# Norm's products of w_o's two parts and of the state space output placed some units further on in PE's order; norm of tokens on DVE alone

## The chip, the cores and the metric

The kernel runs on one NeuronCore of a Trainium2 chip. Its engines work beside each other, each on a queue of its own in a fixed order: PE (matrix products, out of PSUM, the accumulator memory), DVE (vector operations), ACT (activations and copies), POOL (a second vector engine), SP (here: DMA issue). They meet in semaphores. The metric is device time of one execution in microseconds (us). Three runs of the kernel before gave 1786.41, 1787.78 and 1782.34; the median is 1786.41.

## What is computed

One step of a decoder layer for 1024 prompt tokens and 32 sample tokens (1056 columns, T): a mixer with a state space part, cross-attention to 256 memory tokens, and a gated FFN, each with an RMS norm ahead. What matters here:

```python
def rmsnorm(x, g):
    xf = x.astype(F32)
    var = jnp.mean(xf * xf, axis=-1, keepdims=True)
    return (xf * lax.rsqrt(var + EPS) * g.astype(F32)).astype(x.dtype)
...
    y = rmsnorm(y * jax.nn.silu(z.astype(F32)), norm_g)          # state space output
...
    h = h + jnp.concatenate([ya, yb, yc], axis=-1) @ W['w_out'][l]
    h = h + mem_attention(rmsnorm(h, W['norm_mem'][l]), mem_k[l], mem_v[l], W['w_mem_q'][l], W['w_mem_o'][l])
    u = rmsnorm(h, W['norm_ffn'][l])
    h = h + (jax.nn.silu(u @ W['w_ffn_gate'][l]) * (u @ W['w_ffn_up'][l])) @ W['w_ffn_down'][l]
```

All in float32. A product of float32 matrices is made of three products of float32r parts: each operand is split into a high part (ACT copies it) and a low part (DVE subtracts), and high x high, low x high and high x low are summed in PSUM.

## The kernel before

Activations lie with the 1024 features on the partitions (8 tiles `h` of 128 x 1056) and the tokens along the row, so a token's sum of squares runs over partitions. An RMS norm is therefore made on PE in two steps with DVE between. **pv**: the squares, summed over the eight tiles into `acc`, are multiplied by a column of ones, which gives one column of sums per 128 tokens. DVE and ACT turn these into `nr`, 1/rms (`newton`: a root on ACT, a reciprocal and four small operations on DVE). **pb**: `nr` is broadcast by PE transposes, and ACT copies the result to `rbc`, which the activations are multiplied with.

PE and SP execute in the order in which the program is written; ACT, DVE and POOL are put in order by a scheduler when the program is built, and that order is fixed from then on. Where side work stands in PE's order is set by a clock of its own: `tick()` is called at fixed points of the product loops, and a generator that was handed to `spawn` goes on after as many ticks as the number that it yields. In the loop over w_out a unit of 24 matmuls is two ticks; in the loop over w_o's second part a unit of 12 matmuls is two ticks; in the first gate tile 12 matmuls of `st` are one tick.

Three norms are concerned.

- The state space output (`rstd`, L192, called at L879). Its factor is applied after the product with w_out: `z_pairs` are multiplied by w_out unscaled, and `evac` (L901) multiplies what comes out by `rbc`. All three column groups (c = 0, 1, 2; 352 columns) make pv together, two ticks after the loop begins, and pb some ticks later. `nv`, `nr` and `nq` come from the pool `sp`, which has two buffers of each.
- The FFN's norm, first half of the columns of both halves of the tokens (`normed(0, ...)`, L1169). It runs beside the second half of w_o's second part: the loop of L1288 adds units of 12 matmuls to h (`mm`, evacuated by DVE at L1296, three PSUM buffers), squares h on ACT (L1299) and sums on POOL (L1300).
- The same for the second half (`normed(1, ...)`, from `beside`, L1435). It runs beside the first tile of gate and up (L1440 and on): PE makes eight products `st`, four on the first half (c = 0), then four on the second, 48 matmuls each, from `X`, the split, normalised activations. The last two of four are multiplied to `tm` by DVE (L1462).

`normed` goes through four quarters k. For each, ACT scales two tiles of h by the norm's gain (L1175), `un` is multiplied by `rbc` (L1176: one tile on DVE, one on POOL), and `pair` splits the result into x (L1163 on ACT, L1164 on DVE). The first gate tile needs x of all four quarters within its first 12 matmuls, of each half anew. `sums` (L1186) then makes, on DVE and ACT, the sums that the next tiles need: these use a Strassen scheme with seven products (B11, T2, B21, T3, T1, T4, B22). The weights for all this are split on ACT and DVE too (L1258, L1259).

Of the kernel before, what the change touches and what calls it, by code (L numbers as in the profile page):

```python
# [12 lines left out]
OP = mybir.AluOpType  # L13
# [46 lines left out]
def hybrid_step(ctx, tc, xT, memT, consts_d, masks_d, wbd_d, poolw_d, spool_d, w_kv, w_xbc, w_dt, w_lg, w_pool, w_z, h0_d,  # L60
                w_out1, w_out2, w_q, kc_d, vc_d, w_o, w_gu, w_down,
                yT, ktT, vN, smallo, pssd, sssd):
    nc = tc.nc
# [11 lines left out]
    def nm(s):  # L75
        cnt[0] += 1
        return f"{s}{cnt[0]}"

    def slot(dt=F32, name="s"):
        return sl.tile([P, T], dt, tag="slot", name=nm(name))  # L80
# [5 lines left out]
    def spawn(gen):  # L86
        step(gen)

    def step(gen):
        n = next(gen, None)  # L90
        if n is not None:
            heapq.heappush(queue, (now[0] + n, next(order), gen))
# [6 lines left out]
    def drain():  # L99
        while queue:  # L100
            tick()
# [3 lines left out]
    def mmps():  # L105
        return ps.tile([P, CW], F32, tag="mm", name=nm("mm"), bufs=3)

    def smps(shape=(P, 512), name="sm"):
        return ps.tile(list(shape), F32, tag="sm", name=nm(name), bufs=sm_bufs)
# [37 lines left out]
    def unit(out, w, xs, cols, kk):  # L147
        whi, wlo = w
        for k in range(kk):
            a, b = k * P, k * P + P  # L150
            xh, xl = xs[k]
            nc.tensor.matmul(out, whi[:, a:b], xh[:, cols], start=k == 0, stop=False)  # L152
            nc.tensor.matmul(out, whi[:, a:b], xl[:, cols], start=False, stop=False)  # L153
            nc.tensor.matmul(out, wlo[:, a:b], xh[:, cols], start=False, stop=k == kk - 1)  # L154
            if k == kk // 2 - 1:
                tick()
        tick()

    def ch(c):
        return slice(c * CW, (c + 1) * CW)  # L160
# [7 lines left out]
    def cc(name, i=None, n=1):  # L168
        a, b = COFF[name]
        return cst[:, a:b] if i is None else cst[:, a + i:a + i + n]  # L170
# [10 lines left out]
    def newton(r, v, q):  # L181

        nc.scalar.activation(q, v, AF.Sqrt)
        nc.vector.reciprocal(r, q)
        nc.vector.tensor_tensor(q, r, r, op=OP.mult)
        nc.vector.tensor_tensor(q, q, v, op=OP.mult)
        nc.vector.tensor_scalar(q, q, -0.5, 1.5, op0=OP.mult, op1=OP.add)
        nc.vector.tensor_tensor(r, r, q, op=OP.mult)
# [3 lines left out]
    def rstd(c, acc, rbc, n0=0, n1=2):  # L192

        ready[c] = False
        yield n0
        pv = smps(name="pv")
        w = (P, P, CW - 2 * P)
        for t in range(3):
            nc.tensor.matmul(pv[:w[t], t:t + 1], acc[:, t * P:t * P + w[t]], ones[:, :1], start=True, stop=True)
        v = sp.tile([P, 3], F32, tag="nv", name=nm("nv"))  # L200
        r = sp.tile([P, 3], F32, tag="nr", name=nm("nr"))
        q = sp.tile([P, 3], F32, tag="nq", name=nm("nq"))
        nc.gpsimd.memset(v, 1.0)
        nc.vector.tensor_scalar(v[:, :2], pv[:, :2], 1.0 / DM, EPS, op0=OP.mult, op1=OP.add)
        nc.vector.tensor_scalar(v[:w[2], 2:], pv[:w[2], 2:3], 1.0 / DM, EPS, op0=OP.mult, op1=OP.add)
        newton(r, v, q)
        yield n1
        pb = smps(name="pb")
        for t in range(3):
            nc.tensor.transpose(pb[:, t * P:t * P + w[t]], r[:w[t], t:t + 1].to_broadcast([w[t], P]), ident[:w[t], :w[t]])  # L210
        nc.scalar.activation(rbc[:, ch(c)], pb[:, :CW], AF.Copy)
        ready[c] = True
# [137 lines left out]
    for m in range(8):  # L350
        beside(m)
        pk = ps.tile([P, 256], F32, tag="mm", name=nm("pk"), bufs=3)
        unit(pk, kvw[m], mpairs, slice(0, 256), KD)
        kt = tp.tile([P, 256], F32, tag="cy", name=nm("kt"), bufs=5, padded_shape=[P, CY])
        nc.scalar.activation(kt, pk, AF.Copy)
        nc.scalar.dma_start(ktT[m * P:(m + 1) * P, :], kt)
# [477 lines left out]
    z_acc = []  # L834
# [38 lines left out]
    rbc = rp.tile([P, T], F32, tag="rbc", name="rbc_ssd")  # L873
# [2 lines left out]
    h = [bp.tile([P, T], F32, tag="h", name=nm("h"), bufs=8) for _ in range(8)]  # L876
    nc.sync.dma_start(h[0], xT[:P])
    for c in range(NCH):
        spawn(rstd(c, z_acc[c], rbc, 2, 2))  # L879
    ypairs = []  # L880

    def reload():
# [49 lines left out]
    with ExitStack() as at:  # L932
# [193 lines left out]
        rbc = rp.tile([P, T], F32, tag="rbc", name="rbc_ffn")  # L1126
# [5 lines left out]
    def both(t, c):  # L1132

        return t.rearrange("p (s t) -> p s t", s=2)[:, :, c * HB:(c + 1) * HB]

    def rstd2(c):

        pv = smps(name="pv")
        cuts = [(2 * s + i, s * TH + c * HB + i * P, P) for s in range(2) for i in range(2)]
        cuts += [(4 + s, s * TH + c * HB + 2 * P, HB - 2 * P) for s in range(2)]  # L1140
        for i, a, n in cuts:
            nc.tensor.matmul(pv[:n, i:i + 1], acc[:, a:a + n], ones[:, :1], start=True, stop=True)
        v, r, q = (sp.tile([P, 6], F32, tag=t, name=nm(t)) for t in ("nv", "nr", "nq"))
        nc.gpsimd.memset(v, 1.0)
        nc.vector.tensor_scalar(v[:, :4], pv[:, :4], 1.0 / DM, EPS, op0=OP.mult, op1=OP.add)
        nc.vector.tensor_scalar(v[:HB - 2 * P, 4:], pv[:HB - 2 * P, 4:6], 1.0 / DM, EPS, op0=OP.mult, op1=OP.add)
        newton(r, v, q)
        yield 2
        for s in range(2):
            pb = smps(name="pb")  # L1150
            a0 = s * TH + c * HB
            for i, a, n in cuts:
                if a0 <= a < a0 + HB:
                    nc.tensor.transpose(pb[:, a - a0:a - a0 + n], r[:n, i:i + 1].to_broadcast([n, P]), ident[:n, :n])
            nc.scalar.activation(rbc[:, a0:a0 + HB], pb[:, :HB], AF.Copy)
# [6 lines left out]
    def pair(hi, lo, src):  # L1162
        nc.scalar.activation(hi, src, AF.Copy)  # L1163
        nc.vector.tensor_tensor(lo, src, hi.bitcast(F32), op=OP.subtract)  # L1164

    def four(t):
        return t.rearrange("p (s t) -> p s t", s=4)

    def normed(c, n0, n1):  # L1169
        yield n0  # L1170
        yield from rstd2(c)
        for k in range(4):
            UN[k, c] = u4 = four(slot(name="un"))
            for j in range(2):
                nc.scalar.activation(u4[:, 2 * j:2 * j + 2], both(h[k + 4 * j], c), AF.Copy, scale=cc("gffn", k + 4 * j))  # L1175
                (nc.gpsimd if j else nc.vector).tensor_tensor(u4[:, 2 * j:2 * j + 2], u4[:, 2 * j:2 * j + 2], both(rbc, c),  # L1176
                                                              op=OP.mult)
            for j in range(2):
                x = four(slot(F32R, "x"))
                pair(x[:, :2], x[:, 2:], u4[:, 2 * j:2 * j + 2])  # L1180
                for i in range(2):
                    X[f"B{j + 1}{i + 1}", k, c] = x[:, i], x[:, 2 + i]
            if n1 and k < 3:
                yield n1
# [26 lines left out]
    def hold():  # L1211

        m = len(held)
        if m % 2 == 0:
            hold.at = [(wp if m < 4 else fp).tile([P, DM], F32R, tag=t if m < 4 else "b" + t, name=nm(t), bufs=2) for t in ("whi", "wlo")]
        hi, lo = (t[:, m % 2 * 512:m % 2 * 512 + 512] for t in hold.at)
        split_into(w_o[1, m], 512, hi, lo)
        held.append((hi, lo))
# [45 lines left out]
    def fetch():  # L1264
        x = next(gen, None)
        if x is not None:
            batches.append(x)
        return x
# [19 lines left out]
    for c in range(2):  # L1288
        for m in range(8):
            while len(held) < min(m + 2, 8):  # L1290
                hold()
            for s in range(2):
                cols = slice(s * TH + c * HB, s * TH + (c + 1) * HB)
                p = mmps()[:, :HB]
                unit(p, held[m], op1, cols, 4)
                nc.vector.tensor_tensor(h[m][:, cols], h[m][:, cols], p, op=OP.add)  # L1296
            if m:
                sq = fp.tile([P, 2, HB], F32, tag="sq2", name=nm("sq"), bufs=2)
                nc.scalar.activation(sq, both(h[m], c), AF.Square)  # L1299
                nc.gpsimd.tensor_tensor(both(acc, c), both(acc, c), sq, op=OP.add)  # L1300
            else:
                nc.scalar.activation(both(acc, c), both(h[m], c), AF.Square)
            if c and m % 2:
                fetch()
            if c:
                nc.scalar.dma_start(h_dram[:, m, :], h[m])
        if c == 0:
            spawn(normed(0, 4, 6))
    drain()
    ps_.close()  # L1310
    sm_bufs = 2
# [121 lines left out]


    def beside():  # L1435
        yield from normed(1, 2, 1)
        yield 1
        yield from sums(0, 2)
        yield from sums(1, 2)
# [286 lines left out]
```

## Time and profile before

| | |
|---|---|
| median of three runs | 1786.41 us |
| the profiled execution | 1788.4 us |
| its span, first to last instruction | 1786.6 us |
| mean granted clock of PE | 0.99 |
| POOL's mults at L1176, between 1030 and 1081 us | 8, of 1.32 to 1.85 us each |

A row of the timeline gives start, duration, engine, line, operation, output tile and inputs; in square brackets the idle time of the engine before it and what ended it. A row of the waits gives who waited for whom, total us, times and the longest. A row of the windows gives the stretch, its length, busy time (and instructions) of PE, PE's weight loads, DVE, ACT and POOL, PE's granted clock, and the DMA share and rate.

### The profile page before, as it was taken

The page shows a single profiled execution, that of the slowest core. Times are in us where ns is not written, and L with a number is a line of the kernel's source. Part 1 is how long each engine was busy: PE and PEld are TensorE (multiplying, and loading weights), DVE is VectorE, ACT ScalarE, POOL GpSimd, SP SyncE. Part 2 cuts the span into 40 slices and gives each one's busy share as a digit, 9 for nine tenths or more (in the row PEclk, how much of TensorE's full clock was granted, in tenths as well). Part 3 has the DMA queues.
Part 4 walks back from the last instruction along what each step waited for, and adds up shares of the span by engine and source line. Part 5 has one row for each costly group of instructions (what it writes and reads, how often), then busy time and mean ns, then how long its engine had stood idle before and what let it go on. Part 6 is the DMA issues. An engine that isn't in the chain of part 4 may idle for free.

```text
span 1786.6 us, 31851 instructions
## 1 busy us (share of the span) xinstructions
PE 1723.3 (96%) x12307; PEld 1672.8 (94%) x12307; DVE 1131.4 (63%) x2045; ACT 811.7 (45%) x1650; POOL 593.1 (33%) x618
## 2 busy tenths in 40 slices
PE   8899999999999999999999989999999999899997
PEld 7799988888999999999999979999999999899896
DVE  4887877676844534455566479555555556786855
ACT  6546665678634313245565255222322224343344
POOL 2312446554232322212221243433343332211435
PEclk9999999999999999999999989999999999999998
DMA  9112123341320522233344230233322224543322
GB/s 344 68 48 68 65 70 92 107 145 57 125 83 31 210 84 84 79 131 121 116 140 165 90 144 32 85 115 107 105 100 91 96 90 170 199 164 112 118 72 98
DMA packets 106503, 197.51 MB, mean 111 GB/s; under 512 B 15344, under 2 KB 33392, under 8 KB 106352
## 3 DMA queue, kind: packets, MB, share of 16 engines
q1 hardware_dynamic: 94832, 173.54, 28.6%
q10 hardware_dynamic: 11520, 21.94, 3.3%
q8 instruction: 97, 1.59, 0.4%
q14 instruction: 54, 0.44, 0.1%
HBM read 151.54 MB, written 43.89 MB: 109 GB/s over the span
## 4 chain that ended last, share of the span: by engine, by line
PE 77%; DVE 10%; ACT 4%; issue 3%; POOL 3%; DMA 3%; SPq 0%; ACTq 0%; DVEq 0%; POOLq 0%
PE mm L152 12%; PE mm L154 12%; PE mm L153 12%; PE st L1325 10%; PE st L1326 10%; PE st L1327 10%; DVE cy L503 1%; PE poa L1082 1%; PE pss L1064 1%; ACT seg L558 1%; DVE xd L1371 1%; PE st L1453 1%; PE st L1455 1%; PE st L1454 1%; DMA xd<-hid_dram 1%
## 5 line engine op out<-in xcount | busy, mean ns | idle before, releaser
L152 PE MATMUL mm<-uh,whi 128*128 128x352 f32 x960 | 321.1, 334 | 1.1 <-ACT cy L501 1.1
L1325 PE MATMUL st<-x,whi 128*128 128x264 f32 x1120 | 318.9, 285 | 1.0 <-ACT tm L1505 0.5
L1326 PE MATMUL st<-x,whi 128*128 128x264 f32 x1120 | 318.1, 284 | 0.0
L1327 PE MATMUL st<-x,wlo 128*128 128x264 f32 x1120 | 318.0, 284 | 0.0
L154 PE MATMUL mm<-uh,wlo 128*128 128x352 f32 x960 | 311.1, 324 | 0.0
L153 PE MATMUL mm<-ul,whi 128*128 128x352 f32 x960 | 311.0, 324 | 0.0
L1325 PEld LDWEIGHTS st<-x,whi 128*128 128x128 f32 x1120 | 210.7, 188 | 1.6 <-ACT tm L1505 0.7
L1327 PEld LDWEIGHTS st<-x,wlo 128*128 128x128 f32 x1120 | 210.7, 188 | 0.0
L1326 PEld LDWEIGHTS st<-x,whi 128*128 128x128 f32 x1120 | 210.6, 188 | 0.0
L152 PEld LDWEIGHTS mm<-uh,whi 128*128 128x128 f32 x960 | 182.0, 190 | 5.7 <-issue 1.7
L153 PEld LDWEIGHTS mm<-ul,whi 128*128 128x128 f32 x960 | 182.5, 190 | 2.5
L154 PEld LDWEIGHTS mm<-uh,wlo 128*128 128x128 f32 x960 | 181.7, 189 | 0.0
L1325 PE MATMUL st<-xd,whi 128*128 128x264 f32 x504 | 144.6, 287 | 13.7 <-ACT w L1551 7.1
L1326 PE MATMUL st<-xd,whi 128*128 128x264 f32 x504 | 144.0, 286 | 0.0
L1327 PE MATMUL st<-xd,wlo 128*128 128x264 f32 x504 | 143.7, 285 | 0.0
L1258 ACT ACTIVATE whi<-as 128x512 fp32r<-128x512 f32 (+1 forms) x128 | 74.6, 584 | 139.5 <-PE st L1326 96.3
L1258 ACT ACTIVATE whi<-ar 128x512 fp32r<-128x512 f32 (+1 forms) x104 | 60.8, 588 | 150.4 <-PE st L1326 84.3
L123 ACT ACTIVATE whi<-wraw 128x512 fp32r<-128x512 f32 x128 | 77.5, 627 | 106.2 <-PE mm L153 80.1
L1243 POOL TENSOR_TENSOR as<-ar 128x512 f32<-128x512 f32 (+1 forms) x32 | 53.0, 1655 | 205.8 <-DVE wlo L1259 181.6
L124 DVE TENSOR_TENSOR wlo<-wraw,whi 128x512 fp32r<-128x512 f32 x128 | 96.0, 767 | 23.6 <-ACT whi L123 23.5
L1325 PEld LDWEIGHTS st<-xd,whi 128*128 128x128 f32 x504 | 95.6, 190 | 15.2 <-ACT w L1551 7.3
L957 POOL TENSOR_TENSOR kvlo<-kvraw,kvhi 128x512 fp32r<-128x512 f32 x32 | 41.4, 1295 | 163.2 <-ACT kvhi L956 125.3
(460 smaller groups left out, 4437.6 us busy)
## 6 DMA issues: line engine op xcount, KB each, us to landing
ar<-w_gu SPq DMA_DIRECT2D x88, 256.0 KB, 4.1
hid_dram<-tm SPq DMA_DIRECT2D x71, 264.0 KB, 2.1
xd<-hid_dram SPq DMA_DIRECT2D x63, 264.0 KB, 4.9
ar<-w_down SPq DMA_DIRECT2D x48, 192.0 KB, 3.2
h_dram<-h ACTq DMA_DIRECT2D x16, 528.0 KB, 3.0
h<-h_dram SPq DMA_DIRECT2D x16, 528.0 KB, 6.3
seg<-acs_dram SPq DMA_DIRECT2D x32, 256.0 KB, 3.9
wraw<-w_out SPq DMA_DIRECT2D x32, 256.0 KB, 3.6
```

Source lines behind the costliest of these rows:

```text
L123: nc.scalar.activation(hi[:, a:b], raw, AF.Copy)
L124: nc.vector.tensor_tensor(lo[:, a:b], raw, hi[:, a:b].bitcast(F32), op=OP.subtract)
L152: nc.tensor.matmul(out, whi[:, a:b], xh[:, cols], start=k == 0, stop=False)
L153: nc.tensor.matmul(out, whi[:, a:b], xl[:, cols], start=False, stop=False)
L154: nc.tensor.matmul(out, wlo[:, a:b], xh[:, cols], start=False, stop=k == kk - 1)
L503: nc.vector.scalar_tensor_tensor(y[:, :n], raw[:, j:j + n], w[j], y[:, :n], op0=OP.mult, op1=OP.add)
L957: eng.tensor_tensor(lo, src, hi.bitcast(F32), op=OP.subtract)
L1243: nc.gpsimd.tensor_tensor(s1, a21, a22, op=OP.add)
L1258: nc.scalar.activation(hi[:, a], src, AF.Copy)
L1325: nc.tensor.matmul(out, whi[:, a:b], xh, start=begins and k == 0, stop=False, skip_group_check=True)
L1326: nc.tensor.matmul(out, whi[:, a:b], xl, start=False, stop=False, skip_group_check=True)
L1327: nc.tensor.matmul(out, wlo[:, a:b], xh, start=False, stop=k == kk - 1, skip_group_check=True)
```

## The change

`rstd` of the state space output is called with 4 ticks between pv and pb instead of 2. `rstd2` takes that number as a new argument n, 2 for the second half and 5 for the first, where it was 2 for both. The first half's quarters are written 5 ticks apart instead of 6; the second half begins after 4 ticks instead of 2. All mults by `rbc` in `normed` are on DVE.

```diff
-        spawn(rstd(c, z_acc[c], rbc, 2, 2))
+        spawn(rstd(c, z_acc[c], rbc, 2, 4))
...
-    def rstd2(c):
+    def rstd2(c, n):
...
         for i, a, n in cuts:
             nc.tensor.matmul(pv[:n, i:i + 1], acc[:, a:a + n], ones[:, :1], start=True, stop=True)
...
         newton(r, v, q)
-        yield 2
+        yield n
...
     def normed(c, n0, n1):
         yield n0
-        yield from rstd2(c)
+        yield from rstd2(c, 2 if c else 5)
...
-                (nc.gpsimd if j else nc.vector).tensor_tensor(u4[:, 2 * j:2 * j + 2], u4[:, 2 * j:2 * j + 2], both(rbc, c),
-                                                              op=OP.mult)
+                nc.vector.tensor_tensor(u4[:, 2 * j:2 * j + 2], u4[:, 2 * j:2 * j + 2], both(rbc, c), op=OP.mult)
...
-            spawn(normed(0, 4, 6))
+            spawn(normed(0, 4, 5))
...
-        yield from normed(1, 2, 1)
+        yield from normed(1, 4, 1)
```

The loop over `cuts` in `rstd2` has n among its variables; its last cut is (5, ..., HB - 2 * P), with HB = 264 and P = 128.

Three places show how the built order moves. Lines from L1177 on are one less in the changed kernel (L1453 becomes L1452).

PE, first gate tile, before: the products `st` of the first half of the columns, with pv and pb of the second half's norm. pb stands behind the first of four `st`.

```order
L1455 MATMUL st_11704<-x_11608,whi_11442 128x264
L1154 MATMUL pb_11772<-msk,nr_11737 128x128 x2
L1154 MATMUL pb_11772<-msk,nr_11737 128x8
L1154 MATMUL pb_11777<-msk,nr_11737 128x128 x2
L1154 MATMUL pb_11777<-msk,nr_11737 128x8
L1453 MATMUL st_11794<-x_11406,whi_11523 128x264
```

The same place after; st_11823 is the third product of four, st_11894 the fourth.

```order
L1454 MATMUL st_11823<-x_11646,wlo_11611 128x264
L1154 MATMUL pb_11872<-msk,nr_11761 128x128 x2
L1154 MATMUL pb_11872<-msk,nr_11761 128x8
L1154 MATMUL pb_11877<-msk,nr_11761 128x128 x2
L1154 MATMUL pb_11877<-msk,nr_11761 128x8
L1452 MATMUL st_11894<-x_11470,whi_11691 128x264
```

pv stood behind 24 matmuls of the tile and stands behind 48 now; pb stood 24 behind pv and stands 96 behind it now. In the loop over w_o pb stood 12 matmuls behind pv and stands 48 behind it.

DVE, end of the loop over w_o, before: the last evacuations of `mm` (L1296), and the mult, the splits of the last quarter's x and the weight splits around them.

```order
L1296 TENSOR_TENSOR h_10200<-h_10200,mm_11628 128x264
L1296 TENSOR_TENSOR h_10200<-h_10200,mm_11642 128x264
L1296 TENSOR_TENSOR h_10201<-h_10201,mm_11660 128x264
L1176 TENSOR_TENSOR un_11600<-un_11600,rbc_ffn 128x528
L1296 TENSOR_TENSOR h_10201<-h_10201,mm_11674 128x264
L1164 TENSOR_TENSOR x_11605<-un_11600,x_11605 128x528
L1164 TENSOR_TENSOR x_11608<-un_11600,x_11608 128x528
```

After; un_11575 is the third quarter, un_11638 the last.

```order
L1176 TENSOR_TENSOR un_11575<-un_11575,rbc_ffn 128x528 x2
L1295 TENSOR_TENSOR h_10201<-h_10201,mm_11660 128x264
L1164 TENSOR_TENSOR x_11580<-un_11575,x_11580 128x528
L1164 TENSOR_TENSOR x_11583<-un_11575,x_11583 128x528
L1258 TENSOR_TENSOR wlo_11611<-ar_11415,whi_11610 128x512 x2
L1295 TENSOR_TENSOR h_10201<-h_10201,mm_11674 128x264
L1191 TENSOR_TENSOR tt_12013<-un_11526,tt_12013 128x264
L1176 TENSOR_TENSOR un_11638<-un_11638,rbc_ffn 128x528 x2
L1164 TENSOR_TENSOR x_11643<-un_11638,x_11643 128x528
L1164 TENSOR_TENSOR x_11646<-un_11638,x_11646 128x528
```

The last evacuation stood behind the last quarter's mult and ahead of its splits; it stands behind the third quarter's splits and two weight splits now, and the last quarter's mults behind it.

DVE, end of the first gate tile, before: the last product with `st` (L1462), and what stood ahead of it.

```order
L1164 TENSOR_TENSOR x_12092<-tt_12139,x_12092 128x264
L1164 TENSOR_TENSOR x_11787<-t_12015,x_11787 128x264
L1164 TENSOR_TENSOR x_12143<-tt_12139,x_12143 128x528
L1164 TENSOR_TENSOR x_11812<-t_12015,x_11812 128x264
L1164 TENSOR_TENSOR x_11835<-t_12015,x_11835 128x264
L1164 TENSOR_TENSOR x_11858<-t_12015,x_11858 128x264
L1462 TENSOR_TENSOR tm_11703<-tm_11703,st_12235 128x2x264
```

After, the same product and the first eleven rows behind it. Five more rows of 264 elements follow up to the split into x_12216 that completes T2's operand.

```order
L1461 TENSOR_TENSOR tm_11703<-tm_11703,st_12226 128x2x264
L1190 TENSOR_TENSOR tt_12176<-un_11907 128x528
L1258 TENSOR_TENSOR wlo_12286<-as_12064,whi_12285 128x512
L1191 TENSOR_TENSOR tt_12176<-un_11907,tt_12176 128x264
L1164 TENSOR_TENSOR x_12180<-tt_12176,x_12180 128x528
L1192 TENSOR_TENSOR t_12133<-un_11907,tt_12176 128x264
L1164 TENSOR_TENSOR x_12141<-tt_12176,x_12141 128x264
L1190 TENSOR_TENSOR tt_12209<-un_11930 128x528
L1190 TENSOR_TENSOR tt_12251<-un_11953 128x528
L1191 TENSOR_TENSOR tt_12209<-un_11930,tt_12209 128x264
L1164 TENSOR_TENSOR x_12213<-tt_12209,x_12213 128x528
L1192 TENSOR_TENSOR t_12133<-un_11930,tt_12209 128x264
```

All sums of the second half stood ahead of the last product; the sums of its last three quarters stand behind it now.

## The prediction

> **What bounds the kernel now.** I read the page first: busy shares and the chain that ended last.
>
> ```profile
> PE 1723.3 (96%) x12307; PEld 1672.8 (94%) x12307; DVE 1131.4 (63%) x2045; ACT 811.7 (45%) x1650; POOL 593.1 (33%) x618
> ...
> PE 77%; DVE 10%; ACT 4%; issue 3%; POOL 3%; DMA 3%; SPq 0%; ACTq 0%; DVEq 0%; POOLq 0%
> ```
>
> PE (the matmul engine) is busy for 96% and makes up 77% of the chain, so a change that only moves things can win or lose only where PE waits. The second view is who PE waited for; of its 31 rows these five lie where the change acts (columns: total us, times, longest).
>
> ```profile
> PE pv L1142 <- POOL acc_mem L1300: 2.7, 1, 2.7
> PE mm L152 <- DVE h L1296: 2.5, 1, 2.5
> ...
> PE pb L210 <- DVE nr L188: 2.1, 1, 2.1
> ...
> PE pb L1154 <- DVE nr L188: 1.4, 1, 1.4
> ...
> PE st L1453 <- DVE h L1296: 0.8, 1, 0.8
> ```
>
> Third, PE's timeline (start, duration), and two stretches with the granted clock (the PEclk column, here 0.57 and 1.00).
>
> ```profile
> 1024.92 1.18 PE L1142 MATMUL pv<-ones,acc_mem 128*128 128x1 f32 x12
> 1026.03 0.39 PE L152 MATMUL mm<-oh,whi 128*128 128x264 f32 x1
> ...
> 1029.19 1.09 PE L1154 MATMUL pb<-msk,nr 128*128 128x128 f32 x6 [1.43 <-DVE nr L188]
> ...
> 1054.53 0.36 PE L1453 MATMUL st<-x,whi 128*128 128x264 f32 x1 [0.78 <-DVE h L1296]
> ...
> 1060.53 1.93 PE L1142 MATMUL pv<-ones,acc_mem 128*128 128x1 f32 x12 [2.72 <-POOL acc_mem L1300]
> ...
> 1063.21 0.42 PE L1453 MATMUL st<-x,whi 128*128 128x264 f32 x1
> 1063.43 0.42 PE L1454 MATMUL st<-x,whi 128*128 128x264 f32 x1
> ...
> 1067.70 1.04 PE L1154 MATMUL pb<-msk,nr 128*128 128x128 f32 x6
> 1068.67 0.39 PE L1453 MATMUL st<-x,whi 128*128 128x264 f32 x1
> ...
> 1109.69 0.29 PE L1325 MATMUL st<-x,whi 128*128 128x264 f32 x1
> ```
>
> ```profile
> 1040.00:1044.00 4.00, 4.00 (x23) 4.00 (x22) 3.70 (x5) 2.96 (x5) 3.30 (x3) 0.57 0.78 305
> 1084.00:1110.00 26.00, 26.00 (x216) 26.00 (x215) 25.84 (x48) 12.72 (x28) 7.58 (x3) 1.00 0.03 12
> ```
>
> Pace: from 1068.67 to 1109.69 lie 144 + 192 = 336 matmuls, 41.02 / 336 = 0.122 us each. At the low clock it is 1063.43 - 1063.21 = 0.22 us. So a wait costs twice: itself, and a low-clock stretch behind it. The 2.46 us wait was followed by four us with 23 matmuls instead of 4.00 / 0.122 = 33, a loss of 10 x 0.122 = 1.2 us. The 2.72 us wait was followed by low clock up to 1067.4: 22 matmuls that cost 0.10 us more each and a pv of 1.93 instead of 1.18, 2.95 us. PE therefore loses, between the second part of w_o and the end of the first gate tile's first half, 1.43 + 2.46 + 1.2 + 0.78 + 2.72 + 2.95 = **11.5 us**. That is the pot that the change can empty. The 2.07 us at L210 is apart.
>
> **The change, part by part.**
>
> *State space norm (L879, 2 to 4).* The three transposes to pb (the broadcast of 1/rms) go behind one more unit of 24 matmuls.
>
> ```profile
> 581.80 0.77 PE L210 MATMUL pb<-msk,nr 128*128 128x128 f32 x6
> 584.64 0.49 PE L210 MATMUL pb<-msk,nr 128*128 128x128 f32 x3 [2.07 <-DVE nr L188]
> ```
>
> ```profile
> 582.38 0.17 DVE L184 RECIPROCAL nr<-nq 128x3 f32<-128x3 f32 x1 [2.08 <-PE pb L210]
> ```
>
> The third part waits for DVE, but DVE itself waited for PE's pb: the pool of nr has two buffers, so the third nr can only be written once the first transpose has read its buffer. The chain starts when pb starts, wherever pb stands. I take 0 (bounds: -2.07 if the wait went after all; +0.9 if the residual splits that the new DVE order puts ahead of the reciprocal are late).
>
> *Where the other products stand.* The diff says 5 and 2 ticks between the sums of squares (pv) and the broadcast (pb), but `for i, a, n in cuts` in rstd2 overwrites its new argument n; the last cut's n is HB - 2P = 8, so both calls yield 8. The rows on the change show it: in the second call pb stands behind the whole third weight tile, 96 matmuls after pv.
>
> *Start of the gate tiles.* The quarters of x are emitted 5 ticks apart instead of 6, which shows in DVE's order alone. pb of the first half goes from 12 to 48 matmuls behind pv: at 1026.03 + 48 x 0.122 = 1031.9, when nr (ready by 1029.2) is long there: 1.43 us gone. But the mults, splits and evacuations behind it (L1176, L1164, L1259, L1296) go through DVE in a fixed order, now with POOL's four mults among them, and PE may not start `st` before DVE's last L1296, as the 0.78 row shows. DVE's rates, and what a POOL operation does to them:
>
> ```profile
> 1034.23 2.46 DVE L1164 TENSOR_TENSOR x<-un,x 128x528 fp32r<-128x528 f32 x2
> ...
> 1084.37 0.70 DVE L1191 TENSOR_TENSOR tt<-un 128x528 f32<-128x528 f32 x1
> 1084.99 0.69 DVE L1462 TENSOR_TENSOR tm<-tm,st 128x528 f32<-128x528 f32 x1
> 1085.61 0.42 DVE L1192 TENSOR_TENSOR tt<-un,tt 128x264 f32<-128x264 f32 x1
> 1085.95 0.70 DVE L1164 TENSOR_TENSOR x<-tt,x 128x528 fp32r<-128x528 f32 x1
> ```
>
> ```profile
> 1034.53 1.59 POOL L1300 TENSOR_TENSOR acc_mem<-acc_mem,sq 128x528 f32<-128x528 f32 x1 [1.90 <-ACT sq L1299]
> ```
>
> Starts lie 0.62 us behind an operation of 528 (0.60 of 512) and 0.34 behind one of 264. Beside POOL, two of 528 took 2.46 instead of 1.32: a POOL operation blocks DVE for about 1.1 us. In the new order the first mult stands behind the evacuation of the fifth unit after pv (PE has it at about 1034.5, DVE is free for it at 1035.1), and from there to the last L1296 stand 14 operations of 528, 4 of 512, 10 of 264: 8.7 + 2.4 + 3.4 = 14.5 us, so 1049.6 at best; with three of POOL's sums of squares between (3.3 us, of which I let 0.6 fall into DVE's own waits) 1052.3. PE is through at 1026.03 + 168 x 0.122 + 1.1 (pb) = 1047.6. So the 2.46 and the 0.78 become one wait of 4.7 us (bounds 2.0 and 6.8, the latter with DVE ending at 1054.4 as before). Behind the last L1296 still stand, for the last quarter of x, one 264, two mults (one before), ACT's split (0.65) and a DVE split: x is ready 2.5 us after it, PE wants it 9 matmuls = 1.1 us in: 1.4 more (1.1 to 2.4). Low clock for this: 2.0 (1.2 to 3.0).
>
> *The second half's pv* goes 24 matmuls further, past POOL's last sum: 2.72 and its 2.95 are gone; POOL has no mults in front of that sum.
>
> *The second half's pb* stands 48 matmuls before the second half begins, where before it stood 336 - 192 = 144. The work between:
>
> ```profile
> 1069.20 0.71 DVE L1176 TENSOR_TENSOR un<-un,rbc_ffn 128x528 f32<-128x528 f32 x1 [4.54 <-ACT rbc_ffn L1155]
> ...
> 1072.43 0.71 DVE L1176 TENSOR_TENSOR un<-un,rbc_ffn 128x528 f32<-128x528 f32 x1
> ...
> 1080.53 2.00 DVE L1164 TENSOR_TENSOR x<-un,x 128x528 fp32r<-128x528 f32 x2 [0.71 <-ACT x L1163]
> ```
>
> The first mult came 1.5 us after pb's start, a quarter each 1072.43 - 1069.20 = 3.2 us, the last quarter's first x at 1081.2, 13.5 us after. With both mults on DVE I count 3.0 a quarter (mult, ACT split, two ACT scalings, next mult; DVE alone needs 2.5), so 12.6. PE wants the last quarter 1.0 + 5.86 + 1.1 = 7.9 us after pb's start: **a new wait of 4.7 us** (3.9 to 5.6) in two pieces of some 2.1 and 2.6, and 1.2 of low clock (0 to 3).
>
> *The next tile's sums.* The order of DVE now has 16 operations between the last gate product (L1462, now L1461) and the last split that T2, the second product of the next tile, needs; before, all of those stood ahead of it.
>
> ```profile
> 1112.22 0.69 DVE L1462 TENSOR_TENSOR tm<-tm,st 128x528 f32<-128x528 f32 x1
> ...
> 1113.44 1.80 DVE L1245 TENSOR_TENSOR as<-as,ar 128x512 f32<-128x512 f32 x1
> ```
>
> ```profile
> 1113.05 5.14 POOL L1424 TENSOR_TENSOR tm<-tm,tm 128x528 f32<-128x528 f32 x3 [1.40 <-DVE tm L1462]
> ```
>
> That product waits for PE's end of the tile, and the sums are queued behind it on DVE, and T2 on PE behind those. Five of 528, one of 512, ten of 264: 3.1 + 0.6 + 3.4 = 7.1, with the product and its hand-off 8.0 us. PE gets there after 45 matmuls, 5.4 us. At least 2.6 us of wait; POOL's three subtractions in the same place (the 1.80 above is one that they delayed by 1.1) add up to 3.7. I take 5.0, nearer to the upper end because those subtractions start on the same product, and 1.2 of low clock (0 to 3).
>
> *Clock.* The trace drops it after waits of 2.46 and 2.72 us, not after 2.07. [...] The rows above speak for the earlier drop, and no run here has such a wait in pieces; I give the rule one chance in ten, within the forecast's case, since it changes the size and not the sign.
>
> **Sum.** After: 4.7 + 1.4 + 2.0 + 4.7 + 1.2 + 5.0 + 1.2 = 20.2 us lost, against 11.5 before: +8.7 us. The profiled execution took 1788.4 us (span 1786.6), 2.0 above the median of the runs, 1786.41. Against its own time that is 1797.1, and against the median **1795**. What PE loses here it does not get back, since it is the bound. SP's order has the same rows as before, so no DMA of its queue moves; POOL only loses the eight mults.
>
> **Rivals.**
> - *No change.* All bounds at their low ends: 2.0 + 1.1 + 1.2 + 3.9 + 1.2 + 2.6 + 0 = 12.0, +0.5: 1787. For it: DVE sits idle before 1034 in the new order, and POOL's mults no longer block it. Against it: POOL's sums do not go away.
> [...]
> - *The change does not do what it says.* It does not: the 8 for 5 and 2. Were the 2 in force, pb would stand 72 matmuls = 8.8 us earlier, the 4.7 + 1.2 would vanish, and the time would be 1789. The printed order rules this out, so it gets no chance.
>
> **Chances.** A run of this kernel tells 0.3% (5.4 us) from nothing. Forecast (slower, 1792 to 1803) 0.63; no change 0.25; faster 0.12. The range: upper bounds 6.8 + 2.4 + 3.0 + 5.6 + 3.0 + 6.3 + 3.0 = 30.1, +18.6, would be 1805; not all come together, so 1803. Below it takes in the case of no change and its spread, 1785, and leaves out the faster case.
>
> **What would show it.** Right: in PE's waits the pv row (2.7) and the L1154 row (1.4) are gone, the L210 row stays at about 2.1; new rows: `st` L1452 waits for L1295 of 4 to 5 us near 1048, for x L1164 or L1163 at the second half, and L1324 to L1326 for x at T2; three low stretches of the clock. Wrong: if DVE's last L1295 ends before 1049, if x of the second half comes less than 3 us late, or if T2 does not wait. The forecast fails first at DVE's pace, which I count operation by operation from the printed order.

## The result and the profile after

| | before | changed |
|---|---|---|
| median of six runs each | 1786.72 us | 1801.44 us |
| profiled execution | 1788.4 us | 1801.62 us |
| its span | 1786.6 us | 1799.8 us |

The changed kernel is slower: the ratio is 1.0094, 95% interval 1.0081 to 1.0107. Forecast was slower, by 8.7 us; the medians lie 14.7 us apart and the ratio makes it 0.0094 x 1786.7 = 16.8 us. L1295, L1324 and L1423 of the changed kernel are L1296, L1325 and L1424 of before.

The page of the changed kernel, its busy shares: PE is busy for the same share of a longer span, and POOL lost eight instructions.

```profile
PE 1727.6 (96%) x12307; PEld 1675.0 (93%) x12307; DVE 1132.2 (63%) x2053; ACT 812.3 (45%) x1650; POOL 581.6 (32%) x610
```

Who PE waited for in the changed kernel, the main rows in the region of the change (total us, times, longest):

```profile
PE st L1324 <- ACT x L1163: 5.4, 2, 3.0
...
PE st L1452 <- DVE h L1295: 4.2, 1, 4.2
PE pb L210 <- DVE nr L188: 3.4, 1, 3.4
...
PE st L1453 <- DVE x L1164: 2.1, 3, 0.8
PE st L1452 <- ACT x L1163: 2.0, 2, 1.4
...
PE mm L152 <- DVE h L1295: 0.4, 1, 0.4
```

The rows for pv (2.7) and for pb at L1154 (1.4) are gone, as forecast. In their place stand waits of 4.2 at the start of the gate tiles, 3.3 in four pieces at the second half, and 6.8 in three pieces at the next tile. L210 grew from 2.1 to 3.4. The timeline of PE, changed kernel, shows where each stands:

```profile
582.96 0.77 PE L210 MATMUL pb<-msk,nr 128*128 128x128 f32 x6
587.09 0.82 PE L210 MATMUL pb<-msk,nr 128*128 128x128 f32 x3 [3.36 <-DVE nr L188]
...
1053.67 0.47 PE L1452 MATMUL st<-x,whi 128*128 128x264 f32 x1 [4.23 <-DVE h L1295]
1056.90 0.59 PE L1453 MATMUL st<-x,whi 128*128 128x264 f32 x1 [0.78 <-DVE x L1164]
...
1084.56 0.39 PE L1452 MATMUL st<-x,whi 128*128 128x264 f32 x1 [0.62 <-ACT x L1163]
1085.74 0.39 PE L1453 MATMUL st<-x,whi 128*128 128x264 f32 x1 [0.79 <-DVE x L1164]
1087.65 0.40 PE L1452 MATMUL st<-x,whi 128*128 128x264 f32 x1 [1.40 <-ACT x L1163]
1088.56 0.59 PE L1453 MATMUL st<-x,whi 128*128 128x264 f32 x1 [0.50 <-DVE x L1164]
...
1119.95 0.39 PE L1324 MATMUL st<-x,whi 128*128 128x264 f32 x1 [3.02 <-ACT x L1163]
1121.73 0.39 PE L1325 MATMUL st<-x,whi 128*128 128x264 f32 x1 [1.39 <-DVE x L1164]
1124.73 0.59 PE L1324 MATMUL st<-x,whi 128*128 128x264 f32 x1 [2.42 <-ACT x L1163]
```

The wait of 4.2 ends behind DVE's last evacuation:

```profile
1053.10 0.42 DVE L1295 TENSOR_TENSOR h<-h,mm 128x264 f32<-128x264 f32 x1
```

At each of these four places the clock was low. The trace records the granted clock; these are the low stretches that it has there (columns: stretch, length, PE busy with its instructions, granted clock, DMA share, GB/s):

```profile
586.13:592.96 6.83, 5.87 (x21) 0.50 0.75 275
1053.76:1060.59 6.83, 6.05 (x27) 0.50 0.51 198
1087.89:1091.30 3.41, 2.91 (x13) 0.50 0.02 5
1122.02:1128.85 6.83, 4.42 (x19) 0.50 0.49 153
```

In the rest of each stretch PE still waits. At the low clock a matmul takes 0.22 us instead of 0.122 (the wider ones behind L210 0.29 instead of 0.16), so 0.44 of the busy time is lost: 2.6 us behind L210, then 2.7, 1.3 and 1.9 us.

Where the 13.2 us between the two spans came from, by the start of the same instruction in both profiled executions:

| from | to | before | changed | difference | forecast |
|---|---|---|---|---|---|
| start | pv of the state space norm (L199) | 576.1 | 573.4 | -2.7 | 0 |
| | pv of the norm ahead of attention (L251) | 194.4 | 198.3 | **+3.9** | 0 |
| | first pv of the FFN's norm (L1142) | 254.4 | 254.1 | -0.3 | 0 |
| | first product of the next tile (L1324) | 84.8 | 86.2 | +1.4 | +2.5 |
| | first product of the down stage | 410.6 | 419.6 | **+9.0** | +6.2 |
| | end | 266.3 | 268.2 | +1.9 | 0 |

The forecast's +2.5 is 8.1 + 5.9 - 11.5, and its +6.2 is 5.0 + 1.2. The first and the last row hold work that the change does not touch: over all profiled runs the L199 pv began between 573.4 and 577.6, and the last stretch took 265.9 to 269.3. So the first tile came out a little better than forecast, and two terms were too small: L210 (taken as 0) and the next tile.

### The profile page after: what moved, and what is told of

It is laid out like the page before. It is cut to its first block, busy times and chain, and to the rows that moved or that the text cites. A ratio compares the mean times of both kernels' runs of the same rounds, so it can differ in the third digit from the quotient of the medians.

```text
span 1799.8 us, 31843 instructions
## 1 busy us (share of the span) xinstructions
PE 1727.6 (96%) x12307; PEld 1675.0 (93%) x12307; DVE 1132.2 (63%) x2053; ACT 812.3 (45%) x1650; POOL 581.6 (32%) x610
## 5 line engine op out<-in xcount | busy, mean ns | idle before, releaser
L1324 PE MATMUL st<-x,whi 128*128 128x264 f32 x1120 | 319.9, 286 | 5.9 <-ACT x L1163 5.4
L1325 PE MATMUL st<-x,whi 128*128 128x264 f32 x1120 | 319.2, 285 | 1.4 <-DVE x L1164 1.4
L1324 PEld LDWEIGHTS st<-x,whi 128*128 128x128 f32 x1120 | 211.5, 189 | 6.8 <-ACT x L1163 5.9
L1325 PEld LDWEIGHTS st<-x,whi 128*128 128x128 f32 x1120 | 211.4, 189 | 1.9 <-DVE x L1164 1.9
L1324 PE MATMUL st<-xd,whi 128*128 128x264 f32 x504 | 145.9, 289 | 13.0 <-ACT w L1550 7.0
L1325 PE MATMUL st<-xd,whi 128*128 128x264 f32 x504 | 145.2, 288 | 0.0
L1242 POOL TENSOR_TENSOR as<-ar 128x512 f32<-128x512 f32 (+1 forms) x32 | 53.9, 1685 | 230.7 <-DVE wlo L1258 185.1
L1324 PEld LDWEIGHTS st<-xd,whi 128*128 128x128 f32 x504 | 96.9, 192 | 14.6 <-ACT w L1550 7.2
L1326 PEld LDWEIGHTS st<-xd,wlo 128*128 128x128 f32 x504 | 96.8, 192 | 0.0
```

What stands on the lines that cost most here:

```text
L1242: nc.gpsimd.tensor_tensor(s1, a21, a22, op=OP.add)
L1324: nc.tensor.matmul(out, whi[:, a:b], xh, start=begins and k == 0, stop=False, skip_group_check=True)
L1325: nc.tensor.matmul(out, whi[:, a:b], xl, start=False, stop=False, skip_group_check=True)
L1326: nc.tensor.matmul(out, wlo[:, a:b], xh, start=False, stop=k == kk - 1, skip_group_check=True)
```

## The experiments

Ratios are to the kernel before. Eleven kernels ran.

**State space norm put back.** Changed kernel, one edit:

```diff
-        spawn(rstd(c, z_acc[c], rbc, 2, 4))
+        spawn(rstd(c, z_acc[c], rbc, 2, 2))
```

> The changed kernel with the broadcast of the state space norm back at 2 units (L879), all else as changed. Theory 'longer chain': in the changed kernel two w_out evacuations stand on DVE between the Newton steps of the third part, PE waits 3.4 us at L210 instead of 2.1 and is at the low clock behind it; put back, the wait is 2.0 to 2.2, the clock from 580 to 600 us is 1.00, and the time falls by 3 to 4 us, to a ratio to the kernel before of 1.0072 to 1.0078 (changed kernel 1.0094). Rival 'repaid': what PE loses at L210 it does not lose at the next waits, and the ratio stays at 1.0088 to 1.0100.

Measured: 1.0071 (1.0055 to 1.0088). From the L199 pv to the L251 pv it took 194.4 us again, 3.9 less than the changed kernel. PE there:

```profile
583.18 0.49 PE L210 MATMUL pb<-msk,nr 128*128 128x128 f32 x3 [2.07 <-DVE nr L188]
```

The granted clock from 580 to 600 us is 1.00, where it was 0.83 in the changed kernel. By the ratios the longer chain and its clock cost about 0.0023 or 4 us, with intervals of some 3 us on either side; this run's interval just reaches the rival's 1.0088. The rows show the cost at its place. In the profiled execution half of it, 2.1 us, came back up to the down stage, not as waits but as low clock: 6.83 us at the second half and 10.24 at the next tile, where the changed kernel had 3.41 and 6.83.

**Own buffers for the three parts.** The same place from the other side: the norm stays at 4, but the third part's reciprocal no longer waits for a buffer.

```diff
-        r = sp.tile([P, 3], F32, tag="nr", name=nm("nr"))
+        r = sp.tile([P, 3], F32, tag=f"nr{c}", name=nm("nr"), bufs=1)
```

(nv and nq likewise.)

> The changed kernel with buffers of its own for each of the three parts of the state space norm (nr, nv, nq), so that the third reciprocal need not wait for PE's first transpose; all else as changed. Theory 'buffer': the chain at L210 starts at pb because of the buffer alone; with buffers of its own the third nr is ready before pb, the wait of 3.4 us and its low clock go altogether, and the ratio to the kernel before is 1.006 (1.0045 to 1.0072). Rival 'DVE's queue': what is late is the Newton steps behind other work on DVE; a wait of 1.2 us or more stays at L210, and the ratio is 1.0075 to 1.0094.

Measured: 1.0069 (1.0050 to 1.0088). All nine transposes of pb run without a wait; the next wait of PE is 0.5.

```profile
585.18 1.08 PE L210 MATMUL pb<-msk,nr 128*128 128x128 f32 x9
```

So the wait at L210 was the buffer's in both kernels, as the prediction said. How long it lasts is DVE's affair, as the prediction did not say. DVE in the changed kernel:

```profile
582.86 1.29 DVE L124 TENSOR_TENSOR wlo<-wraw,whi 128x512 fp32r<-128x512 f32 x2
584.06 0.17 DVE L184 RECIPROCAL nr<-nq 128x3 f32<-128x3 f32 x1
584.15 0.49 DVE L903 TENSOR_TENSOR ev<-mm,rbc_ssd 128x352 f32<-128x352 f32 x1
584.56 0.15 DVE L185 TENSOR_TENSOR nq<-nr 128x3 f32<-128x3 f32 x1
584.63 0.52 DVE L903 TENSOR_TENSOR ev<-mm,rbc_ssd 128x352 f32<-128x352 f32 x1
585.06 0.75 DVE L186 TENSOR_TENSOR nq<-nq,nv 128x3 f32<-128x3 f32 x1
585.85 0.90 DVE L187 TENSOR_SCALAR nq<-nq 128x3 f32<-128x3 f32 x1
586.78 0.16 DVE L188 TENSOR_TENSOR nr<-nr,nq 128x3 f32<-128x3 f32 x1
```

The same chain in the kernel before, from the second small step on, and POOL in the changed kernel:

```profile
582.89 0.53 DVE L903 TENSOR_TENSOR ev<-mm,rbc_ssd 128x352 f32<-128x352 f32 x1
...
583.40 0.52 DVE L903 TENSOR_TENSOR ev<-mm,rbc_ssd 128x352 f32<-128x352 f32 x1
583.83 0.67 DVE L188 TENSOR_TENSOR nr<-nr,nq 128x3 f32<-128x3 f32 x1
```

```profile
584.86 1.81 POOL L904 TENSOR_TENSOR h<-h,ev 128x352 f32<-128x352 f32 x2 [7.55 <-DMA wraw<-w_out]
```

Two evacuations stand inside the chain in both kernels (in the kernel before, L186 starts at 582.78 and L187 at 583.33, each ahead of one of them). They are not what made it longer. Two things differ. The reciprocal, behind two residual splits, starts 1.1 us behind pb (582.96) instead of 0.58. And the evacuations now come early enough that POOL's additions of the evacuated units (L904) stand beside two of the small steps, L186 and L187, which take 0.75 and 0.90 us; in the kernel before they stand beside one, L188, which takes 0.67. The other small steps take 0.15 to 0.17. From the reciprocal's start to the end of L188 it is 2.88 us instead of 2.12. POOL's two additions end at 585.80 and 586.68, L186 and L187 at 585.81 and 586.74; that POOL is the cause is read from these times, and no run took the additions away.

**POOL's mults back.** Changed kernel, with L1176 alternating between DVE and POOL as before:

```diff
-                nc.vector.tensor_tensor(u4[:, 2 * j:2 * j + 2], ..., both(rbc, c), op=OP.mult)
+                (nc.gpsimd if j else nc.vector).tensor_tensor(u4[:, 2 * j:2 * j + 2], ..., both(rbc, c), op=OP.mult)
```

> The changed kernel with every second multiplication by the norm (L1176) on POOL again, all positions as changed. Theory 'position': the waits of the second half and of the next tile's T2 come from where the second half's pb stands; the T2 wait stays at 5 us or more, and the ratio at 1.007 to 1.012. Rival 'DVE's load': four more multiplications on DVE in each half are what makes T2 late; the T2 wait falls below 3 us and the ratio below 1.005.

Measured: 1.0091 (1.0074 to 1.0108). The next tile still waits 5.2 + 1.2 = 6.4 us for x. Ahead of the gate tiles PE waits 2.1 and 3.4 us for evacuations instead of 0.4 and 4.2. In the changed kernel, who multiplies does not matter to the time.

**DVE's mults alone.** The kernel before with the opposite of that edit, positions as before.

> The kernel before with all multiplications by the norm on DVE, all positions as before. Theory 'position': the pb of the second half stands as early as before, so there is no wait in the second half and T2 waits less than 1 us; the ratio is 0.998 to 1.002. Rival 'DVE's load': a wait of 3 us or more at T2 or at the start of the gate tiles, and a ratio of 1.003 or more.

Measured: 0.9990 (0.9981 to 1.0000). The longest of PE's waits from 1015 to 1150 us:

```profile
PE pv L1142 <- POOL acc_mem L1299: 2.7, 1, 2.7
```

The 2.5 us that PE waited for evacuations became 0.4. A part of this is the clock's: it was low from 1030.1 to 1033.6 us here, so that PE came some 1.5 us later. The run with pv further on, below, has the mults on DVE and a granted clock of 1.00 from 1020 to 1040 us, and PE waits 0.26 and 0.39 us; so POOL's mults had held up DVE. No wait appears at the next tile. The wait of pv for POOL's last sum stays at 2.7 although POOL no longer multiplies.

**The gap as the change writes it.** Changed kernel; rstd2's argument keeps its value, so that 5 and 2 ticks stand between pv and pb instead of 8.

```diff
-    def rstd2(c, n):
+    def rstd2(c, n0):
...
-        yield n
+        yield n0
```

> The changed kernel with rstd2's argument under a name that its loop does not overwrite, so that 5 and 2 units stand between pv and pb instead of 8. Theory 'position': the second half's pb stands 72 matmuls earlier, the 3.3 us of waits and the low clock there are gone, T2 waits less than 3.5 us instead of 6.8; about 11 us less than the changed kernel, a ratio of 1.002 (1.000 to 1.005). Rival 'DVE's load': only the second half's waits go, T2 still waits 5 us or more, and the ratio is 1.005 to 1.007.

Measured: 1.0011 (1.0001 to 1.0020), 15 us below the changed kernel by the ratios. No wait for x is left at the second half or the next tile, and the wait at the start of the gate tiles is 2.4 us. Two others are new there:

```profile
PE st L1324 <- ACT tm L1478: 1.9, 1, 1.9
PE st L1324 <- DVE tm L1480: 1.8, 1, 1.8
```

**Only the second half's gap.** Changed kernel with 8 in the first half and 2 in the second:

```diff
-        yield n
+        yield 8 if c == 0 else 2
```

> The changed kernel with 8 units between pv and pb in the first half (as it has) and 2 in the second. Theory 'the second half's place is most of it': the 3.3 us in the second half and the 6.8 us at T2 are gone with their low clock, the 4.2 us at the start of the gate tiles stays; about 12 us less than the changed kernel, a ratio of 1.002 to 1.004. Rival 'first half': the first half's late start makes the sums late too; T2 still waits 3 us or more, and the ratio is 1.005 or more.

Measured: 1.0019 (1.0007 to 1.0031). The waits of 3.3 and 6.8 us for x are gone, the 4.2 at the start stays, and at the next tile stand 1.9 at L1478 and 0.4 at L1480.

This one place, pb 72 matmuls too late, is worth 1.0094 - 1.0019 = 0.0075 or 13 us: most of the loss. (The ratio lies just below the expected 1.002 to 1.004.) The first half's gap of 8 instead of 5 is worth 1.0019 - 1.0011, or 1.4 us, within the intervals.

**POOL's subtractions off POOL.** What makes the wait at the next tile 6.8 and not 5.0? Changed kernel, the first tile's four subtractions (L1423) on DVE, where they come to stand behind the sums:

```diff
-                nc.gpsimd.tensor_tensor(t, x, y, op=sub)
+                (nc.gpsimd if f else nc.vector).tensor_tensor(t, x, y, op=sub)
```

> The changed kernel with the four subtractions of the first tile (L1423) on DVE, where they stand behind the last split of the sums, instead of on POOL. Theory 'POOL blocks DVE at T2': three subtractions on POOL each hold up DVE by 1.1 us among the sums; without them the wait at T2 is 2.5 to 4.0 us instead of 6.8, though a wait at L1478 or L1480 of up to 2 us may come behind it; ratio 1.006 to 1.009. Rival 'DVE's own work': the sums take as long without POOL; T2 waits 5.5 us or more, and the ratio is 1.009 or more.

DVE and POOL in the changed kernel, behind the last gate product:

```profile
1115.97 1.81 DVE L1258 TENSOR_TENSOR wlo<-as,whi 128x512 fp32r<-128x512 f32 x1
1117.71 1.52 DVE L1191 TENSOR_TENSOR tt<-un,tt 128x264 f32<-128x264 f32 x1
1119.15 1.83 DVE L1164 TENSOR_TENSOR x<-tt,x 128x528 fp32r<-128x528 f32 x1
```

```profile
1115.61 4.82 POOL L1423 TENSOR_TENSOR tm<-tm,tm 128x528 f32<-128x528 f32 x3 [6.71 <-DVE tm L1461]
```

The same three on DVE without POOL beside them, and PE's waits there:

```profile
1117.60 0.68 DVE L1258 TENSOR_TENSOR wlo<-as,whi 128x512 fp32r<-128x512 f32 x1
1118.20 0.42 DVE L1191 TENSOR_TENSOR tt<-un,tt 128x264 f32<-128x264 f32 x1
1118.55 0.69 DVE L1164 TENSOR_TENSOR x<-tt,x 128x528 fp32r<-128x528 f32 x1
```

```profile
1119.98 0.39 PE L1325 MATMUL st<-x,whi 128*128 128x264 f32 x1 [0.17 <-DVE x L1164]
1122.98 0.39 PE L1324 MATMUL st<-x,whi 128*128 128x264 f32 x1 [2.49 <-ACT x L1163]
1123.56 0.39 PE L1325 MATMUL st<-x,whi 128*128 128x264 f32 x1 [0.19 <-DVE x L1164]
1126.54 0.59 PE L1324 MATMUL st<-x,whi 128*128 128x264 f32 x1 [1.78 <-ACT tm L1478]
```

The wait for x is 0.17 + 2.49 + 0.19 = 2.85 us. So DVE's own queue makes 2.85 of the 6.83 and POOL's subtractions the other 4.0; each of the three held up one DVE operation by 1.1 (1.81 - 0.68, 1.52 - 0.42, 1.83 - 0.69). But the time is 1.0091 (1.0076 to 1.0107), the rival's figure. What was won at x went to a wait of 1.78 us at L1478, which now queues behind the splits, and to more work inside the low clock behind it (PE is busy for 5.1 of the 6.83 us, where it was 4.4). From the next tile's first product to the down stage it took 418.7 us instead of 419.6. The wait's cause is shown; the expected gain in time did not come.

**pv further on, alone.** The kernel with DVE's mults alone, and the second half's pv at 4 ticks, pb still 2 behind it:

```diff
-        yield from normed(1, 2, 1)
+        yield from normed(1, 4, 1)
```

> The kernel before with all multiplications on DVE (the run before this, 0.999) and with the second half's pv 24 matmuls further on, pb still 24 matmuls behind pv. Theory 'position': pv's 2.7 us wait for POOL's last sum and the low clock behind it are gone, pb 240 instead of 264 matmuls ahead of the second half's use costs nothing, T2 waits less than 1.5 us; 4 us less, a ratio of 0.9965 (0.995 to 0.998). Rival 'late anyway': x of the second half or the sums come too late by about as much, with a wait of 2.5 us or more there, and the ratio is 0.9985 to 1.001.

Measured: 0.9981 (0.9971 to 0.9992). Half a miss. pv does not wait any more, and from the first pv to the next tile PE took 76.1 us instead of 81.7. Not all of these 5.6 us are pv's: 2.7 are its wait and 1.5 the low clock behind it, and some 1.5 are the low clock at 1030 us, behind pb, that only the run with DVE's mults alone had. And 4.3 were lost again up to the down stage (413.9 instead of 409.6), at the waits of the gap runs, 1.9 at L1478 and 0.4 at L1480, and a low clock of 3.41 us between them.

**The same with own buffers for nr.**

> The kernel of the run with pv further on, and with buffers of its own for each part of the state space norm at 2 units (L879). Theory 'buffer': the 2.1 us at L210 goes; 2 to 3 us less than without, a ratio of 0.995 (0.9935 to 0.997). Rival 'DVE's queue': the third part's Newton steps then come behind the same work on DVE, 1.2 us or more of wait stay at L210, and the ratio is that of the run without, within 0.0007.

Measured: 0.9970 (0.9960 to 0.9981). The 2.1 us at L210 are gone at 2 ticks too. The wait at L1480 is 1.8 here instead of 0.4, which takes back a part: the low stretch of 3.41 us falls behind that wait here and ahead of it in the run before.

**Quarters at one place.** The waits at L1478 and L1480 come from where the next tile's results lie: in these kernels the first one gets a buffer that POOL's subtractions still read, in the kernel before one that DVE frees. What ACT waits for ahead of L1478 shows it, first with pv further on, then in this run:

```profile
1108.94 0.61 ACT L1478 ACTIVATE tm<-st 128x528 f32<-128x528 f32 x1 [3.32 <-POOL tm L1423]
```

```profile
1100.10 0.61 ACT L1478 ACTIVATE tm<-st 128x528 f32<-128x528 f32 x1 [1.50 <-DVE x L1164]
```

With the second half's quarters written at one place the first buffer is again DVE's. POOL's next weight sums (L1242) then also stand between the subtractions again, as in the kernel before; this run does not part the two.

```diff
-        yield from normed(1, 4, 1)
+        yield from normed(1, 4, 0)
```

> The kernel of the last run (own buffers, pv further on) with the four quarters of the second half's x emitted at one place instead of one unit apart. The next tile's first gate result (L1478) then takes a buffer that DVE gives free, as in the kernel before, and no longer one that POOL's subtractions (L1423) still read. Theory 'buffer of tm': the waits of 1.9 (ACT tm L1478) and 1.8 us (DVE tm L1480) in the next tile and their low clock are gone; 3 to 5 us less, a ratio of 0.9945 (0.9935 to 0.996). Rival 'POOL's subtractions': they delay DVE there in any case, 2 us or more of wait stay in the next tile, and the ratio is 0.997 to 0.998.

Measured: 0.9952 (0.9933 to 0.9971), 1776.89 us: the best of all, ahead of both kernels. PE's waits from 1015 to 1150 us are all of these:

```profile
PE pb L1154 <- DVE nr L188: 1.4, 1, 1.4
PE mm L152 <- DVE h L1295: 0.6, 2, 0.4
PE st L1452 <- DVE h L1295: 0.6, 1, 0.6
PE st L1324 <- DVE tm L1480: 0.4, 1, 0.4
```

From the next tile to the down stage it took 410.7 us, 5.3 less than the run before it.

**One tick more ahead of the first half's pb.** That kernel, with a gap of 3 in the first half:

```diff
-        yield 2
+        yield 2 if c else 3
```

> The run above with one place for the quarters, and 3 units between the first half's pv and pb instead of 2. Theory 'nr in time': the 1.4 us wait at pb is gone and the gate tiles start with 0.6 to 1.2 us of wait; the ratio is up to 0.0007 below that run's. Rival 'passed on': what pb no longer waits for is waited for at the start of the gate tiles (2 us or more there), and the ratio is that run's or up to 0.001 above.

Measured: 0.9967 (0.9954 to 0.9979). The rows speak for the rival: pb's wait fell from 1.4 to 0.7, and behind it DVE is late with the evacuations, by 2.0 us in the loop over w_o and 1.8 at the start of the gate tiles. The ratio is 0.0015 above that run's, more than the rival said, but the two intervals overlap.

```profile
PE mm L152 <- DVE h L1295: 2.0, 2, 1.3
PE st L1452 <- DVE h L1295: 1.8, 1, 1.8
```

## Why the prediction was right in its direction and too small

**The pot.** The rows for pv and L1154 are gone, as forecast. The kernel with pv alone further on shows that this part is a gain of its own. Its size, put at 2.72 + 2.95, is 2.7 + 1.5 there. Behind the same wait the clock was low for 6.83 us in the kernel before, and for 3.41 with DVE's mults alone, against which that run is measured.

**Start of the gate tiles.** Forecast 4.7 + 1.4 + 2.0 = 8.1. Measured 4.23 + 0.78 of waits and 2.7 of low clock, 7.7, and 0.4 at an evacuation. DVE's pace, counted operation by operation, held, and the run with a gap of 3 shows the same mechanism in small.

**The second half.** Forecast 4.7 + 1.2 in two pieces. Measured 3.3 in four pieces and 1.3 of low clock. The run with 8 and 2 shows that pb's place alone makes it.

**The next tile: the first term that failed.** The step was: "I take 5.0, nearer to the upper end because those subtractions start on the same product, and 1.2 of low clock". The two ends were right: "at least 2.6" was 2.85 without POOL, and POOL's "3.7" was 4.0. But the three subtractions fell into the sums one by one, so the terms add in full; 6.3 should have been taken. Measured 6.83 and 1.9, that is 8.7 against 6.2.

**L210: the second.** The step was: "The chain starts when pb starts, wherever pb stands. I take 0". That it hangs on pb's start is right, and the run with own buffers confirms why. The step took what follows that start as fixed. It is made of DVE operations in a fixed order, and what else is ready beside them changes with the place. One unit later the reciprocal came 0.5 us later behind two residual splits, inside the bound of +0.9 that the prediction had set for them, and the small steps behind it took 0.8 us longer, two of them beside POOL's additions instead of one. The wait grew by 1.3. The low clock behind it, for which nothing had been set, cost 2.6. Together 3.9, as by the stretches. The runs with the mults on POOL, with gaps of 5 and 2 and of 8 and 2, and with the subtractions on DVE wait as long at L210, 3.3 to 3.5 us, with a low stretch of 3.41 us behind it instead of 6.83; from the L199 pv to the L251 pv they take 197.2 to 197.4 us, 2.7 to 3.0 more than the kernel before. So about 1 us of the 3.9 belongs to this execution.

**Sum.** With these sizes: 3.9 + (7.7 + 0.4 + 4.6 - 11.5) + 8.7 = 13.8 us, against 13.2 between the spans and 14.7 between the medians. The +8.7 of the forecast lacked 3.9 at L210 and 2.5 at the next tile, and was 1.3 too high in the first tile. That the sum comes so close is in part luck: a low stretch of 3.41 us costs up to 0.44 x 3.41 = 1.5 us, and at the same place the runs differ by one such stretch. At the second half the changed kernel has 3.41 us of it and the run with the state space norm put back 6.83, behind the same four waits; at the next tile 6.83 and 10.24.

**The rivals.** "Faster", given 0.12, needed DVE at its last L1295 before PE was through, counted at 1047.6; DVE started there at 1053.1. "No change" fell at the start of the gate tiles (a wait of 4.2 us where it needed 2.0) and at the next tile (6.8 where it needed 2.6). The case that had no chance, the 5 and 2 in force, was priced at 1789; run, it gave 1787.9 us. That it fits is luck, because errors cancelled in that price: the wait at the next tile went as well and the one at the start of the gate tiles fell to 2.4 us, and 1.9 and 1.8 us at tm and 3.5 at L210 came.

**The clock.** The one chance in ten, within the forecast's case, was for waits in pieces that cost no clock. At the second half, pieces of at most 1.40 us, 3.3 in all, were followed by 3.41 us of low clock. The clock's loss, 4.4 forecast in all, was 8.5 us.

## What to carry to other kernels

Where a small chain on a shared engine sits between two products, its length is not a constant to move about: ask what else becomes ready beside it at the new place. A product placed later to meet its input is paid for by everything behind it that it feeds; here 72 matmuls at one pb were worth 13 us, while the move of pv with its gap kept short cost no wait for the x behind it. And when several bounded delays start on the same event and stand in one queue, add them.

## What the runs showed of the hardware

The low clock did not follow from the length of the wait alone. PE waited 2.07 us at L210 in the kernel before, with state space norm put back, with DVE's mults alone and with pv further on. Only in the third of these did the clock fall, 1.3 us after the wait had ended at 585.06; in the kernel before it was 1.00 from 584.6 to 592.0 us. With DVE's mults alone:

```profile
586.00:596.00 10.00, 10.00 (x55) 0.83 0.75 259
```

In the trace's record of the clock of the kernel before and of the changed kernel, every low stretch but the one that ends each execution is 3.41 us long or twice or three times that, and within one execution their starts lie whole multiples of 3.413 us apart: in the kernel before the clock falls at 340.48, 773.97, 1040.21 and 1060.69, which is 127 (433.49 us, 3.413 each), 78 and 6 of them; in the changed kernel at 586.13, 1053.76, 1087.89 and 1122.02, which is 137, 10 and 10. Counted in steps of 3.413 us from where the clock falls in each run (in the kernel before at 1040.21; with state space norm put back at about 1084.5, with DVE's mults alone at 586.4 and with pv further on at 1110.9, where PE's matmuls turn slow), the 2.07 us lie within one step where the clock fell (583.00 to 586.41), and a bound between two steps cuts them in the three others, into 0.25 + 1.82, 1.68 + 0.39 and 0.19 + 1.88. That this decides is not shown: the 1.43 us at L1154 lie within one step in the kernel before and with DVE's mults alone, and only in the latter was the clock low behind them (1030.1 to 1033.6).

In the changed kernel each DVE operation beside one of POOL's three subtractions took about 1.1 us longer than without them, as the three pairs of rows above show (1.81, 1.52 and 1.83 us against 0.68, 0.42 and 0.69), and ended only after the subtraction: these end at 1117.2, 1118.9 and 1120.4 us, and the DVE operations 0.3 to 0.6 us later.
